# Two attention branches on one core: the second branch's third score pass as pairs of 64-row matmuls

## The chip, the cores and the metric

The kernel runs on one core of a Trainium2 chip. The metric is the device time of one execution in microseconds (us), the median of several runs. A core has a matrix engine (TensorE, PE in the profile), three engines for elementwise work (VectorE = DVE, ScalarE = ACT, GpSimd = POOL) and SyncE (SP), whose queue issues all of this kernel's copies (DMAs). Engines run side by side and wait for each other through semaphores. TensorE multiplies a stationary tile of up to 128 rows by 128 columns, put into its array by a weight load (PEld), with a moving tile of up to 512 columns, and adds the products in PSUM, in banks of 512 fp32 columns.

## What is computed

One encoder layer for 2048 prompt tokens and 512 sample tokens of width 1024. A wide input projection feeds two attention branches of eight heads each; both are gated, projected, merged and projected again (the tail). What the change touches is the second branch:

```python
qb = (rms_norm(bq, b_q_g) @ b_q_up).reshape(bsz, n, B_HEADS, B_NOPE + B_ROPE)
qb = concatenate([qb[..., :B_NOPE], apply_rope(qb[..., B_NOPE:], cos_b, sin_b)], axis=-1)
kv = (rms_norm(bkv, b_kv_g) @ b_kv_up).reshape(bsz, n, B_HEADS, B_NOPE + B_V)
kr = apply_rope(bkr.reshape(bsz, n, 1, B_ROPE), cos_b, sin_b)
kb = concatenate([kv[..., :B_NOPE], broadcast_to(kr, (bsz, n, B_HEADS, B_ROPE))], axis=-1)
vb = kv[..., B_NOPE:]
yb = block_attention(qb, kb, vb, (B_NOPE + B_ROPE) ** -0.5)
```

A key of this branch has 64 numbers of its own head and 32 (`kr`) shared by all heads. Each softmax is exact, with the row's maximum taken off.

## The kernel before, in words

Numbers are kept as pairs of a high part (rounded to the fp32r format; such a matmul has one record in the trace) and a low part (the rest), and a product is the sum of high x high, high x low and low x high.

**Stages.** `in_proj` (to about 1150 us) projects all tokens and stores q, k, v and gates. `attention` works through 80 jobs, `specs`: branch, head, chunk of 512 queries (four prompt chunks with 2048 keys, then one sample chunk with 512). `tail` does the rest. The first branch's jobs end at about 1944 us, the second's scores run from there to 2771.

**A job** is worked through in pairs of key tiles, 128 keys each: eight pairs for a prompt chunk, two for a sample chunk, so 272 pairs in each branch. For each pair `scores` (L969 to L989) takes a PSUM tile `st` of two banks (two such tiles exist), one bank for each key tile, and adds up 512 columns in each bank:

- first branch, two passes of 128 rows: `k1` x `qm`, `k2` x `qz`;
- second branch, three passes of 128 rows (L916): `k2` x `qm`, `k1` x `q1`, `k3` x `qz`.

In the third pass `k3` holds the high part of `kr` in rows 0 to 31, -1 in row 64 and zeros elsewhere; `qz` holds the low part of the query's rotary numbers in rows 0 to 31 and the query's maximum in row 64. So 33 of its 128 rows do work. ScalarE then takes the exponential twice (L983 rounded to `ph`, L984 in place), VectorE the difference `pl` (`lows`, L993), GpSimd adds up `ph` for the sums (L986). `values` (L996 to L1009), two steps later, multiplies `ph` and `pl` with the values `vt` (L1003, L1004), two matmuls for each key tile. `finish` copies the results out; VectorE's L1027 frees the bank for the next job's values.

**Maxima.** `max_stream` (L933 to L967) runs 12 to 13 steps ahead of the scores: for each step two matmuls `mp` (L947) and a reduction on VectorE (L950); at the end of a job a transpose (L959), and one step later `row` (L961) writes the maxima into row 64 of the job's `qz` by four small copies. That is some four steps ahead of the job's first scores.

**Order.** From L972 on, the order of every engine is written out by hand (`manual_schedule`). One step of the loop issues: the six (or four) score matmuls of a pair, one key tile (`values`), one step of the maxima, the second key tile, copies that are due, and `lows`. In a usual step of the second branch TensorE gets 6 + 2 + 4 = 12 matmuls. Copies go through SyncE's one queue in the order of issue; `later(n, f)` puts one off by n steps. `start_main` (L905) loads a job's `q1` and `qz` one or two jobs ahead, `load_k` (L801) the keys and values of a head five jobs ahead for the prompt. `k3` is loaded once for each of the two lengths (L826, L827), its memsets (L780, L781) run in the projection stage, and three `qz` are used in turn by both branches.

**Matmuls of fewer rows.** Two helpers in the projection stage, L264 and L464, multiply 4-row tiles with a 4x2 tile in plain fp32, each with two records in the trace; all other matmuls but one use all 128 rows. `sel[0]` x `acc` (L1008), at the end of each prompt job, is plain fp32 with 128 rows.

Of the kernel before, what the change touches and what calls it, by code (L numbers as in the profile page):

```python
# [10 lines left out]
F32R = mybir.dt.float32r  # L11
# [6 lines left out]
P = 128  # L18
# [14 lines left out]
def emit(tc, x_prompt, x_sample, c_prompt, c_sample, ada_w, ada_b, pre_g, post_g, w_in,  # L33
# [55 lines left out]
    with dram_cm as dram, const_cm as const:  # L89
# [27 lines left out]
        env = locals()  # L117
        h4 = in_proj(tc, nc, env)
        wt = attention(tc, nc, env, h4)
        tail(tc, nc, env, wt)  # L120

# [637 lines left out]
def attention(tc, nc, env, h4):  # L759
    e = NS(env)  # L760
    dma, nm, f32 = e.dma, e.nm, e.f32
    ha, fl, filler, cur, rest = h4
    kp = Pool(tc, "kp", "left")
# [12 lines left out]
        kv[0].append(kv_tiles(kp, NP_TOK, i))  # L776
    k3s = []
    for n in (NP_TOK, NS_TOK):
        k3 = kp.tile([P, n], F32R, name=f"k3{n}")
        nc.gpsimd.memset(f32(k3), 0.0)  # L780
        nc.gpsimd.memset(f32(k3[64:65, :]), -1.0)  # L781
        k3s.append(k3)
    qzs = []

# [16 lines left out]
    def load_k(br, kvh, smp, post):  # L801

        key = (br, kvh, smp)
        if key in kcur:
            return
        t0, n = (NP_TOK, NS_TOK) if smp else (0, NP_TOK)
        sl = slice(t0, t0 + n)
        k1, k2, vt = kv[smp][kcur["n"][smp] % len(kv[smp])]
        kcur["n"][smp] += 1
        rows = slice(64 * (kvh % 2), 64 * (kvh % 2) + 64)  # L810
        if br == 0:
            for s in range(2):
                post(k1[64 * s:64 * s + 64, :], e.ak_s[s][rows, sl])
            post(k2[0:64, :], e.ak_s[0][rows, sl])
            vsrc = e.va_s[sl, kvh, :]
        else:
            post(k2[0:64, :], e.bkn_s[0][kvh // 2, rows, sl])
            for s in range(2):
                post(k2[64 + 32 * s:96 + 32 * s, :], e.kr_s[s][:, sl])
            for s in range(2):  # L820
                post(k1[64 * (1 - s):64 * (1 - s) + 64, :], e.bkn_s[s][kvh // 2, rows, sl])
            vsrc = e.vb_s[sl, kvh, :]
        vsrc = vsrc.rearrange("(t p) d -> p t d", p=P)
        for t in range(0, n // P, 4):
            post(vt[:, t:t + 4, 0:P], vsrc[:, t:t + 4, :])
        if br == 1 and ("k3", smp) not in kcur:  # L826
            post(k3s[smp][0:32, :], e.kr_s[0][:, sl])  # L827
            kcur["k3", smp] = True
        kcur[key] = (k1, k2, vt)

# [6 lines left out]
    def q_src(br, h, c):  # L837
        sl = slice(c * CH, (c + 1) * CH)
        rows = slice(64 * (h % 2), 64 * (h % 2) + 64)
        return [s[h // 2, rows, sl] for s in (e.aq_s if br == 0 else e.bqn_s)], \  # L840
            [s[32 * h:32 * h + 32, sl] for s in e.bqr_s]

    def start(i, br, h, c):

        j = Job()
        j.br, j.h, j.c = br, h, c
        j.last = (br, h, c) == specs[-1]
        smp = int(c == 4)
        j.nk = (NS_TOK if smp else NP_TOK) // P
        j.direct = 0 if smp else j.nk // 2 - 1  # L850
        j.k1, j.k2, j.vt = kcur[(*kv_of(br, h), smp)]
        j.k3 = k3s[smp]
        qn, qr = q_src(br, h, c)
        j.qz = qzs[i % 3]
        j.qm = kp.tile([P, CH], F32R, tag="qm", name=nm("qm"), bufs=4)
        if br == 0:
            dma(f32(j.qm), qn[0].partition_broadcast(2))
            j.km = j.k1
            j.scale = SC_A
        else:  # L860
            dma(f32(j.qm[0:64, :]), qn[0])
            dma(f32(j.qm[64:128, :]), qr[0].partition_broadcast(2))
            j.km = j.k2
            j.scale = SC_B
        j.mx = kp.tile([P, 4, 2], F32, tag="mx", name=nm("mx"), bufs=3)
        return j
# [5 lines left out]
    def first():  # L872
        pieces = []
        load_k(0, 0, 0, lambda out, in_: pieces.append(lambda: post_now(out, in_)))

        def query():
            started[0] = start(0, 0, 0, 0)

        return pieces + [query]
# [5 lines left out]
    def mp_bank():  # L885
        return pp.tile([P, 2, CH], F32, tag="mp", name=nm("mp"), bufs=1)
# [18 lines left out]
    def start_main(i, br, h, c):  # L905

        qn, qr = q_src(br, h, c)
        qz = qzs[i % 3]
        if br == 0:
            dma(f32(qz[0:64, :]), qn[1])  # L910
            return lambda j, ks: ((j.k1[:, ks], j.qm), (j.k2[:, ks], qz))
        q1 = at.tile([P, CH], F32R, tag="q1", name=nm("q1"), bufs=3)
        for s in range(2):
            dma(f32(q1[64 * s:64 * s + 64, :]), qn[s])
        dma(f32(qz[0:32, :]), qr[1])
        return lambda j, ks: ((j.k2[:, ks], j.qm), (j.k1[:, ks], q1), (j.k3[:, ks], qz))  # L916

    jobs = []
    clock = [0]
# [2 lines left out]
    def later(steps, f):  # L922
        queue.append((clock[0] + steps, len(jobs), f))
        queue.sort(key=lambda q: q[0])
# [5 lines left out]
    def ahead(i):  # L930
        started[i] = start(i, *specs[i])

    def max_stream():  # L933

        for i, sp in enumerate(specs):
            j = started.pop(i, None) or start(i, *sp)
            jobs.append(j)
            long = j.nk > 4
            for n in range(pairs[i]):
                if n == 3 and i + 1 < len(specs):  # L940
                    ahead(i + 1)
                if n == 6 and i + 2 < len(specs) and pairs[i + 1] < 8:
                    ahead(i + 2)
                mp = mp_bank()
                for a in range(2):
                    qt, kc = (n // 2, 2 * (n % 2) + a) if long else (2 * n + a, 0)
                    nc.tensor.matmul(mp[:, a, :], lhsT=j.qm[:, qt * P:(qt + 1) * P],  # L947
                                     rhs=j.km[:, kc * CH:(kc + 1) * CH], start=True, stop=True)
                if long:
                    nc.vector.tensor_reduce(out=j.mx[:, n // 2, n % 2:n % 2 + 1], in_=mp.rearrange("p a k -> p (a k)"),  # L950
                                            axis=AX.X, op=ALU.max)
                else:
                    nc.vector.tensor_reduce(out=tops[i % 3][0][:, 2 * n:2 * n + 2], in_=mp, axis=AX.X, op=ALU.max)
                if n + 1 < pairs[i]:
                    yield True
            m, mt = tops[i % 3]
            if long:
                nc.vector.tensor_reduce(out=m[:, 0:4], in_=j.mx, axis=AX.X, op=ALU.max)
            nc.vector.transpose(out=mt, in_=m)  # L959

            def row(j=j, mt=mt):  # L961
                r = f32(j.qz[64:65, :]).rearrange("o (t b q) -> o t b q", b=4, q=32)
                for b in range(4):
                    dma(r[:, :, b, :], mt[32 * b:32 * b + 4, :])

            later(1, row)
            yield True  # L967

    def scores(j, n):  # L969

        if n == 0:
            if j.direct:  # L972
                j.acc = at.tile([P, 2, CH], F32, tag="acc", name=nm("acc"), bufs=2)
            j.hs, j.ls = [], []
        st = pp.tile([P, 2, CH], F32, tag="st", name=nm("st"), bufs=2)
        for a in range(2):
            kt = 2 * n + a
            ps = j.passes(j, slice(kt * P, (kt + 1) * P))
            for i, (k, q) in enumerate(ps):
                nc.tensor.matmul(st[:, a, :], lhsT=k, rhs=q, start=(i == 0), stop=(i == len(ps) - 1))  # L980
        h = at.tile([P, 2, CH], F32R, tag="ph", name=nm("ph"), bufs=6)
        j.hs.append(h)
        nc.scalar.activation(out=h, in_=st, func=AF.Exp, scale=j.scale)  # L983
        nc.scalar.activation(out=st, in_=st, func=AF.Exp, scale=j.scale)  # L984
        if 0 < n < j.direct:
            nc.gpsimd.tensor_tensor(out=j.acc, in0=f32(j.hs[0]) if n == 1 else j.acc, in1=f32(h), op=ALU.add)  # L986
            if n == j.direct - 1:
                nc.gpsimd.tensor_tensor(out=j.acc[:, 0, :], in0=j.acc[:, 0, :], in1=j.acc[:, 1, :], op=ALU.add)
        return st  # L989
# [55 lines left out]
    with contextlib.ExitStack() as order:  # L1045
# [12 lines left out]
        ha.close()  # L1058
        wt = Pool(tc, "wt", "right")
        passes = {0: start_main(0, *specs[0])}  # L1060
        order.close()
        order.enter_context(tc.manual_schedule(engines={eng.PE, eng.Activation, eng.DVE, eng.Pool, eng.SP}))
        ready, g = [], -1
        while g + 1 < len(steps) or ready:
            g += 1
            clock[0] = g
            st, rest = None, None
            if g < len(steps):
                i, n = steps[g]
# [25 lines left out]
                st = scores(jobs[i], n)  # L1095
                ready += [(g + BACK + (n == 0), jobs[i], 2 * n + a) for a in range(2)]
            now = sum(r[0] <= g for r in ready)
            for m in range(min(now, 3)):
                if m == 1:
                    advance(lead + g + 1)  # L1100
                _, j, kt = ready.pop(0)
# [226 lines left out]
```

## Time and profile before

| | |
|---|---|
| time, median of 3 runs | 3247.29 us (3246.39 to 3251.93) |
| the profiled execution's own time | 3247.96 us |
| its span, first to last instruction | 3246.2 us |
| second branch, first to last score matmul | 826.6 us |

How to read it: a page gives each engine's busy time and the span in 40 equal slices, a digit being the share in tenths (9: 90% or more; PEclk: TensorE's granted clock in tenths of full speed). The other views are taken from the same execution: stretches (after the columns named there come the share and the GB/s of the DMA engines), groups of equal instructions with their mean duration and the idle time ahead of them, waits by the one waited for, and the timeline (start, length, engine, line, operation, out<-in, stationary rows*columns, shape, count, and in brackets the idle time of that engine before it). "PE" is the matmul, "PEld" the weight load, "SPq" an issue by SyncE, "issue" idle time without a semaphore that explains it. A matmul's end is modelled, and matmuls overlap, so its length is longer than the distance to the next.

### The profile page before, as it was taken

What the parts mean: (1) busy time and instruction counts of PE and PEld (TensorE: products, weight loads), DVE (VectorE), ACT (ScalarE), POOL (GpSimd) and SP (SyncE); (2) the same over time, 40 slices, a digit from 0 to 9 for tenths busy, and PEclk for the clock granted to TensorE, in tenths of its full rate; (3) what the DMA queues carried; (4) which work ended last, traced back from release to release, by engine and by line L of the source; (5) the groups of instructions that cost most, each with busy time, mean ns of one, the idle gap of its engine ahead of it and who ended that gap; (6) DMA issues with size and microseconds to landing.
All of it is one profiled execution on the core that took longest, in us unless ns stands there. A gap on an engine that the chain in (4) does not pass through costs nothing. (4 is left out here: it accounts for less than half of the span.)

```text
span 3246.2 us, 41787 instructions
## 1 busy us (share of the span) xinstructions
PE 3150.9 (97%) x15214; PEld 2543.9 (78%) x15214; DVE 1970.9 (61%) x2521; ACT 1635.3 (50%) x2169; POOL 1727.2 (53%) x1044
## 2 busy tenths in 40 slices
PE   7999999999999999999999999999999999999999
PEld 6988889988889777666666677777776777789998
DVE  5742214422206128999999998888888887544343
ACT  5332224232323237777777876766666676421122
POOL 6422123421214237777777777666766667654443
PEclk9999999999999999999999999999999999999999
DMA  8445542355524751012111034432333222565552
GB/s 242 145 153 202 198 144 91 132 192 198 188 91 150 228 148 42 27 32 61 28 40 31 29 80 93 95 83 74 89 83 77 53 70 71 177 188 169 159 174 74
DMA packets 277521, 373.39 MB, mean 115 GB/s; under 512 B 30636, under 2 KB 184564, under 8 KB 274852
## 3 DMA queue, kind: packets, MB, share of 16 engines
q1 hardware_dynamic: 277316, 370.73, 38.3%
q8 instruction: 120, 1.97, 0.3%
q14 instruction: 85, 0.70, 0.1%
HBM read 251.52 MB, written 118.96 MB: 114 GB/s over the span
## 5 line engine op out<-in xcount | busy, mean ns | idle before, releaser
L986 POOL TENSOR_TENSOR acc<-acc,ph 128x1024 f32<-128x1024 f32 x320 | 768.9, 2403 | 89.0 <-ACT ph L983 76.3
L983 ACT ACTIVATE ph<-st 128x1024 fp32r<-128x1024 f32 x544 | 558.3, 1026 | 394.6 <-PE st L980 391.3
L950 DVE TENSOR_REDUCE mx<-mp 128x1 f32<-128x1024 f32 x512 | 625.8, 1222 | 200.5 <-PE mp L947 198.6
L993 DVE TENSOR_TENSOR pl<-st,ph 128x1024 fp32r<-128x1024 f32 x544 | 658.2, 1210 | 32.6 <-ACT st L984 32.6
L984 ACT ACTIVATE st<-st 128x1024 f32<-128x1024 f32 x544 | 555.3, 1021 | 0.0
L209 POOL TENSOR_TENSOR wl<-wraw,wh 128x1536 fp32r<-128x1536 f32 (+3 forms) x59 | 189.0, 3214 | 508.3 <-ACT wh L208 507.7
L980 PE MATMUL st<-qm,k 128*128 128x512 f32 x1024 | 434.6, 424 | 7.1 <-DVE pl L993 6.2
L1003 PE MATMUL pv<-ph,vt 128*128 128x512 f32 x1024 | 406.5, 397 | 29.9 <-DVE s L1027 29.9
L980 PE MATMUL st<-qz,k 128*128 128x512 f32 x1056 | 418.1, 396 | 0.0
L1004 PE MATMUL py<-pl,vt 128*66 128x512 f32 x1024 | 405.8, 396 | 0.0
L947 PE MATMUL mp<-k,qm 128*128 128x512 f32 x1024 | 323.9, 397 | 2.6 <-DVE mx L950 0.4
L604 PE MATMUL mm<-hh,wh 128*128 128x512 f32 x768 | 302.2, 394 | 0.0
L604 PE MATMUL mm<-hl,wh 128*128 128x512 f32 x768 | 301.8, 393 | 0.0
L604 PE MATMUL mm<-hh,wl 128*128 128x512 f32 x768 | 301.8, 393 | 0.0
L980 PEld LDWEIGHTS st<-qm,k 128*128 128x128 f32 x1024 | 194.0, 189 | 104.5 <-DVE pl L993 29.4
L1003 PEld LDWEIGHTS pv<-ph,vt 128*128 128x128 f32 x1024 | 193.5, 189 | 88.0 <-DVE s L1027 36.5
L947 PEld LDWEIGHTS mp<-k,qm 128*128 128x128 f32 x1024 | 190.0, 188 | 80.4 <-DVE mx L950 17.5
L986 POOL TENSOR_TENSOR acc<-ph,ph 128x1024 f32<-128x1024 f32 x64 | 152.9, 2389 | 183.3 <-ACT ph L983 172.3
L980 PEld LDWEIGHTS st<-qz,k 128*128 128x128 f32 x1056 | 200.0, 189 | 48.4 <-issue 7.4
L340 PE MATMUL mm<-wh,hh 128*128 128x384 f32 (+1 forms) x640 | 211.2, 330 | 5.7 <-DVE rp L80 3.9
L340 PE MATMUL mm<-wl,hh 128*128 128x384 f32 (+1 forms) x640 | 210.3, 329 | 0.0
L340 PE MATMUL mm<-wh,hl 128*128 128x384 f32 (+1 forms) x640 | 205.7, 330 | 0.0
(235 smaller groups left out, 5735.3 us busy)
## 6 DMA issues: line engine op xcount, KB each, us to landing
wraw<-in_w_in SPq DMA_DIRECT2D x46, 768.0 KB
x<-in_x_prompt SPq DMA_DIRECT2D x32, 512.0 KB
wada<-in_ada_w SPq DMA_DIRECT2D x24, 512.0 KB
raw<-in_w_in SPq DMA_DIRECT2D x48, 256.0 KB
vb<-uv SPq DMA_DIRECT2D x20, 512.0 KB
qm<-aqh SPq DMA_DIRECT2D x40, 256.0 KB
mt<-ma SPq DMA_DIRECT2D x40, 256.0 KB
mt<-mb SPq DMA_DIRECT2D x40, 256.0 KB
```

The lines of the kernel that those rows point to most:

```text
L209: eng.tensor_tensor(out=l[:, :, 0:n], in0=raw[:, :, 0:n], in1=f32(h[:, :, 0:n]), op=ALU.subtract)
L340: nc.tensor.matmul(ps[:, 0:n], lhsT=lt, rhs=rt, start=(i == 0), stop=(i == 23))
L604: nc.tensor.matmul(ps, lhsT=lt, rhs=rt[:, k, :], start=(i == 0), stop=(i == 23))
L947: nc.tensor.matmul(mp[:, a, :], lhsT=j.qm[:, qt * P:(qt + 1) * P], rhs=j.km[:, kc * CH:(kc + 1) * CH], start=True, stop=True)
L950: nc.vector.tensor_reduce(out=j.mx[:, n // 2, n % 2:n % 2 + 1], in_=mp.rearrange("p a k -> p (a k)"), axis=AX.X, op=ALU.max)
L980: nc.tensor.matmul(st[:, a, :], lhsT=k, rhs=q, start=(i == 0), stop=(i == len(ps) - 1))
L983: nc.scalar.activation(out=h, in_=st, func=AF.Exp, scale=j.scale)
L984: nc.scalar.activation(out=st, in_=st, func=AF.Exp, scale=j.scale)
L986: nc.gpsimd.tensor_tensor(out=j.acc, in0=f32(j.hs[0]) if n == 1 else j.acc, in1=f32(h), op=ALU.add)
L993: nc.vector.tensor_tensor(out=l, in0=st, in1=f32(j.hs[-1]), op=ALU.subtract)
L1003: nc.tensor.matmul(j.X, lhsT=j.vt[:, kt, 0:P], rhs=j.hs[n][:, a, :], start=st, stop=sp)
L1004: nc.tensor.matmul(y, lhsT=j.vt[:, kt, 64:VW], rhs=j.ls[n][:, a, :], start=st, stop=False)
```

## The change

The third pass is cut to 64 rows. `k3` is half as long: rows 0 to 63 hold the even key tiles and rows 64 to 127 the odd ones, each with `kr` in its first 32 rows and -1 in its 33rd. `qz` holds the same query data twice, in rows 0 to 32 and in rows 64 to 96, so there is one more copy of the rotary part and four more of the maxima for each job of the second branch. A pair's order of matmuls becomes: passes one and two of the first tile, passes one and two of the second, third pass of the first (rows 0 to 63), third pass of the second (rows 64 to 127). The first branch has two passes and keeps its order.

```diff
--- before.py
+++ after.py
@@ -776,9 +776,10 @@
         kv[0].append(kv_tiles(kp, NP_TOK, i))
     k3s = []
     for n in (NP_TOK, NS_TOK):
-        k3 = kp.tile([P, n], F32R, name=f"k3{n}")
+        k3 = kp.tile([P, n // 2], F32R, name=f"k3{n}")
         nc.gpsimd.memset(f32(k3), 0.0)
-        nc.gpsimd.memset(f32(k3[64:65, :]), -1.0)
+        for r in (32, 96):
+            nc.gpsimd.memset(f32(k3[r:r + 1, :]), -1.0)
         k3s.append(k3)
     qzs = []
 
@@ -824,7 +825,9 @@
         for t in range(0, n // P, 4):
             post(vt[:, t:t + 4, 0:P], vsrc[:, t:t + 4, :])
         if br == 1 and ("k3", smp) not in kcur:
-            post(k3s[smp][0:32, :], e.kr_s[0][:, sl])
+            tiles = e.kr_s[0][:, sl].rearrange("p (t two k) -> p t two k", two=2, k=P)
+            for a in range(2):
+                post(k3s[smp][64 * a:64 * a + 32, :].rearrange("p (t k) -> p t k", k=P), tiles[:, :, a, :])
             kcur["k3", smp] = True
         kcur[key] = (k1, k2, vt)
 
@@ -908,12 +911,19 @@
         qz = qzs[i % 3]
         if br == 0:
             dma(f32(qz[0:64, :]), qn[1])
-            return lambda j, ks: ((j.k1[:, ks], j.qm), (j.k2[:, ks], qz))
+            return lambda j, kt: [(j.k1[:, kt * P:(kt + 1) * P], j.qm), (j.k2[:, kt * P:(kt + 1) * P], qz)]
         q1 = at.tile([P, CH], F32R, tag="q1", name=nm("q1"), bufs=3)
         for s in range(2):
             dma(f32(q1[64 * s:64 * s + 64, :]), qn[s])
-        dma(f32(qz[0:32, :]), qr[1])
-        return lambda j, ks: ((j.k2[:, ks], j.qm), (j.k1[:, ks], q1), (j.k3[:, ks], qz))
+        for a in range(2):
+            dma(f32(qz[64 * a:64 * a + 32, :]), qr[1])
+
+        def passes(j, kt):
+            ks, half = slice(kt * P, (kt + 1) * P), slice(64 * (kt % 2), 64 * (kt % 2) + 64)
+            n = kt // 2
+            return [(j.k2[:, ks], j.qm), (j.k1[:, ks], q1), (j.k3[half, n * P:(n + 1) * P], qz[half, :])]
+
+        return passes
 
     jobs = []
     clock = [0]
@@ -959,9 +969,10 @@
             nc.vector.transpose(out=mt, in_=m)
 
             def row(j=j, mt=mt):
-                r = f32(j.qz[64:65, :]).rearrange("o (t b q) -> o t b q", b=4, q=32)
-                for b in range(4):
-                    dma(r[:, :, b, :], mt[32 * b:32 * b + 4, :])
+                for p in (64,) if j.br == 0 else (32, 96):
+                    r = f32(j.qz[p:p + 1, :]).rearrange("o (t b q) -> o t b q", b=4, q=32)
+                    for b in range(4):
+                        dma(r[:, :, b, :], mt[32 * b:32 * b + 4, :])
 
             later(1, row)
             yield True
@@ -973,11 +984,12 @@
                 j.acc = at.tile([P, 2, CH], F32, tag="acc", name=nm("acc"), bufs=2)
             j.hs, j.ls = [], []
         st = pp.tile([P, 2, CH], F32, tag="st", name=nm("st"), bufs=2)
-        for a in range(2):
-            kt = 2 * n + a
-            ps = j.passes(j, slice(kt * P, (kt + 1) * P))
-            for i, (k, q) in enumerate(ps):
-                nc.tensor.matmul(st[:, a, :], lhsT=k, rhs=q, start=(i == 0), stop=(i == len(ps) - 1))
+        ps = [j.passes(j, 2 * n + a) for a in range(2)]
+        last = len(ps[0]) - 1
+        order = [(a, i) for a in range(2) for i in range(2)] + [(a, i) for i in range(2, last + 1) for a in range(2)]
+        for a, i in order:
+            k, q = ps[a][i]
+            nc.tensor.matmul(st[:, a, :], lhsT=k, rhs=q, start=(i == 0), stop=(i == last))
         h = at.tile([P, 2, CH], F32R, tag="ph", name=nm("ph"), bufs=6)
         j.hs.append(h)
         nc.scalar.activation(out=h, in_=st, func=AF.Exp, scale=j.scale)
```

## Rows read from the trace of the kernel before

**Rows 1.** the page: TensorE's busy time and share; its granted clock in 40 slices.

```profile
...
PE 3150.9 (97%) x15214; PEld 2543.9 (78%) x15214; DVE 1970.9 (61%) x2521; ACT 1635.3 (50%) x2169; POOL 1727.2 (53%) x1044
...
PEclk9999999999999999999999999999999999999999
...
```

**Rows 2.** stretches, first, second branch: length, busy (count) PE PEld DVE ACT POOL, clock.

```profile
...
1308.00:1944.40 636.40, 618.10 (x2547) 442.76 (x2546) 596.32 (x583) 501.81 (x553) 485.92 (x233) 0.99 0.16 42
...
1944.40:2771.00 826.60, 806.73 (x3394) 603.29 (x3393) 672.58 (x652) 570.14 (x630) 571.51 (x272) 0.99 0.32 78
```

**Rows 3.** who TensorE's matmuls waited for, second branch: us, times, longest.

```profile
...
PE pv L1003 <- DVE s L1027: 14.2, 8, 1.8
PE st L980 <- DVE pl L993: 5.4, 2, 4.8
```

**Rows 4.** costliest groups, second branch: busy, mean ns, idle before, releaser.

```profile
...
L993 DVE TENSOR_TENSOR pl<-st,ph 128x1024 fp32r<-128x1024 f32 x272 | 329.1, 1210 | 25.3 <-ACT st L984 25.3
L950 DVE TENSOR_REDUCE mx<-mp 128x1 f32<-128x1024 f32 x245 | 299.6, 1223 | 116.7 <-PE mp L947 116.1
L983 ACT ACTIVATE ph<-st 128x1024 fp32r<-128x1024 f32 x271 | 278.1, 1026 | 249.6 <-PE st L980 248.2 <-POOL acc L986 0.8 <-POOL acc L988 0.5
...
```

**Rows 5.** timeline, one pair of the second branch: start, length, engine, line.

```profile
...
2203.02 0.39 PE L1003 MATMUL pv<-ph,vt 128*128 128x512 f32 x1
...
2204.41 0.40 PE L980 MATMUL st<-q,k 128*128 128x512 f32 x1
2204.41 0.19 PEld L980 LDWEIGHTS st<-qz,k 128*128 128x128 f32 x1
2204.64 0.39 PE L980 MATMUL st<-qz,k 128*128 128x512 f32 x1
...
2204.87 0.39 PE L1003 MATMUL pv<-ph,vt 128*128 128x512 f32 x1
...
```

**Rows 6.** timeline, gate projection: 512-column matmuls, 4-row ones, and back.

```profile
...
225.78 0.40 PE L604 MATMUL mm<-hl,wh 128*128 128x512 f32 x1
226.10 0.18 PEld L464 LDWEIGHTS tr<-comb,mrow 4*128 4x128 f32 x1 [0.37 <-issue]
226.11 0.27 PE L464 MATMUL tr<-comb,mrow 4*128 4x2 f32 x1
...
227.44 0.52 PEld L464 LDWEIGHTS tr<-comb,mrow 4*128 4x128 f32 x4
...
227.98 0.19 PEld L604 LDWEIGHTS mm<-hh,wl 128*128 128x128 f32 x1
227.98 0.50 PE L604 MATMUL mm<-hh,wl 128*128 128x512 f32 x1
...
228.32 0.40 PE L604 MATMUL mm<-hh,wh 128*128 128x512 f32 x1
...
```

**Rows 7.** timeline, weight loads: two other passages into 4-row matmuls.

```profile
...
31.49 0.52 PEld L264 LDWEIGHTS tr<-comb,row 4*128 4x128 f32 x4 [0.17 <-issue]
...
59.63 0.52 PEld L264 LDWEIGHTS tr<-comb,row 4*128 4x128 f32 x4 [0.17 <-issue]
...
```

**Rows 8.** timeline, end of a job: a 128-row matmul of the other format.

```profile
...
2206.50 0.39 PE L1006 MATMUL py<-ph,sel 128*66 128x512 f32 x1
2206.50 0.36 PEld L1008 LDWEIGHTS py<-acc,sel 128*66 128x66 f32 x2
...
```

**Rows 9.** row and query copies: durations of all; SyncE's timeline; first third pass.

```profile
...
L44 SPq DMA_DIRECT2D qz<-mt x320: 572/573/684, 1203.7 to 2743.8; - x160
...
2293.60 2.56 SPq L44 DMA_DIRECT2D qz<-mt  x4
...
2300.89 0.53 SPq L44 DMA_DIRECT2D qz<-bqrl  x1
...
2303.95 0.40 PE L980 MATMUL st<-qz,k 128*128 128x512 f32 x1
...
```

**Rows 10.** L780: duration in ns, min, median, max; first and last start.

```profile
...
L780 POOL MEMSET k<- x2: 523/1168/1812, 1050.5 to 1052.3; 128x2048 f32 x1, 128x512 f32 x1
...
```

## The prediction

> **What bounds the kernel now.** I read the page first: TensorE is marked busy for 97% of the span, no other engine for more than 61%, and the granted clock is at the top of its scale in every slice [rows 1]. A matmul's end is modelled, so that share alone proves little. Next I cut out the stretch the change touches, from the first score matmul of the second branch (1944.4) to the last (2771.0), and the pure part of the first branch for comparison [rows 2]. The second branch lasts 826.6 us for 8 x (4 x 8 + 2) = 272 pairs of key tiles, 3.04 us each. VectorE is busy 81% of it, ScalarE 69%, GpSimd 69%; in the first branch VectorE stood at 94%.
>
> The waits of TensorE settle it: in those 826.6 us it waited on another engine 10 times, 19.6 us in all [rows 3], while ScalarE waited 248 us for score matmuls and VectorE 116 us for the maxima's [rows 4]. So in the second branch TensorE's own stream sets the pace, and what is added to or taken from it reaches the end almost whole.
>
> The timeline gives the price of one matmul. From 2203.02 to 2204.87 there are eight steps of 512 columns in 1.85 us, 0.231 us each. The duration printed (0.39 to 0.40) is latency; the pitch is what counts. Each weight load starts when the matmul before it starts, and lies wholly beside it [rows 5].
>
> **What the change does to TensorE.** A pair has 12 matmuls of that pitch in its usual step: six scores, two maxima, four values. The change keeps the first two passes, moves both third passes to the end of the six and makes each a 64-row matmul, one on rows 0 to 63, one on rows 64 to 127. Count from the start of the last full score matmul to the start of the value matmul behind the scores.
>
> Before: three steps, 3 x 0.231 = 0.693 us.
>
> After, if the halves run side by side, one matmul of 0.231 goes. But the array passes from 128-row use to 64-row use and back in every pair. The second branch of the kernel before has no such passage, so I looked for matmuls of fewer rows. The nearest are in the input projection: 4-row matmuls straight behind 512-column ones [rows 6]. There the last full matmul starts at 225.78, and its successor would have started at 226.01. The 4-row weight load, which in the ordinary stream would have begun at 225.78, begins only at 226.10: 0.09 us after the columns have gone in, with no semaphore named ("issue"). It then lies bare: the way back shows what a bare load costs, since the full matmul printed at 227.98 is 0.50 long instead of 0.40 and its successor comes 0.34 later instead of 0.23, so 0.11 us. Way in: 0.09 + 0.11 = 0.20 us.
>
> On the way back the 4-row loads follow one another at 0.113 (four loads printed as 0.52 from 227.44, each 0.18 long, so the last begins at 227.78); the full load comes at 227.98, 0.20 behind it and thus 0.09 late, and again lies bare for 0.11. Way out: 0.20 us.
>
> Is it the number of rows, or the switch between the two fp32 formats? Two other passages into 4-row matmuls show the same idle load queue [rows 7], while a 128-row matmul of the other format, at the end of a job, has its load begin with the matmul before it, as usual [rows 8]. So it is the rows.
>
> The Trainium skill, TensorEngine Tiling (Array Packing), Key Properties, says that a change of tiling mode drains the engine. These rows show such a drain for 4 rows; that it also holds for halves of 64 rows no run here shows yet.
>
> Between the two halves there is a second load. On one and the same row block, loads with almost no matmul between them come 0.113 apart [rows 6]. The second half's load stands behind the first half's matmul in the queue, but goes to other rows. Bounds: 0 (it overlaps the first load) and 0.11 (it follows it, while the first half's matmul already runs). I take 0.11, since the only bare loads shown follow one another. The Trainium skill, TensorE: Matmul & The Clock Gate, Part 3, has packed tiles start some 4 ns apart; by that the lower bound would hold and the sum would be 3289.
>
> Sum after: 0.231 (the last full matmul) + 0.20 (in) + 0.11 (second load) + 0.231 (second half's columns) + 0.20 (out) = 0.972 us. Against 0.693 that is **+0.28 us a pair**, x 272 = +76 us; with the lower bound +0.17, or +46.
>
> A little is absorbed. Eight waits of 1.77 us behind the 2-pair jobs, 14.2 us in all [rows 3], are for VectorE; two slower pairs (0.56 us) come before each, so up to 8 x 0.56 = 4 us goes. Result: +72 us (bounds +42 and +72).
>
> **The rest of the edit.** Per second-branch job SyncE issues four more row copies and one more query copy: 4 x 0.573 + 0.53 = 2.8 us, x 40 = 113 us spread over 826. The rows of a job were issued from 2293.60, done at 2296.16, and the job's first third pass ran at 2303.95 [rows 9]. Finishing 2.3 us later leaves 5.5 us, and the third pass now comes later in its pair. Behind the rows stand loads of keys and queries for later jobs, which move by the same 2.8 us: several us to jobs ahead, so nothing. If that cover went, 40 jobs x up to 2.8 us = 113 us would show as TensorE waiting at a job's first pair. The key tile of the third pass is loaded in two copies instead of one, once for each of the two lengths, about 0.5 us of issue each, jobs ahead of its use. Its memset, 1.81 us for 2048 columns, becomes half as long, and the row of -1 becomes two of half the length; GpSimd runs them during the projection, at 1050 to 1055 [rows 10]: nothing either way. The first branch keeps its order, since it has two passes: nothing.
>
> The profiled execution took 3247.96 (span 3246.2 and 1.8 around it), 0.7 above the median of 3247.29. So 3247.3 + 72 = **3319 us**.
>
> **Rivals.**
> (a) The halves of 64 rows are entered and left without a drain: then a pair saves 0.231, 272 pairs save 63 us, and the time is 3185. For it: the load queue otherwise works ahead in every step [rows 5]; VectorE would rise to 672.6 / 764 = 88%, below the 94% it reached in the first branch [rows 2]. Against: rows 6 and 7. It decides as soon as in, out and second load together cost less than 0.231. The packing measurements in TensorE: Matmul & The Clock Gate of the Trainium skill would lead there; they time packs, and what rows 6 show is the passage between full and packed use. Chance 0.14.
> (b) Only the drain of 0.09 is paid each way and the loads are hidden: 0.231 + 0.09 + 0.231 + 0.09 = 0.642, that is -0.05 a pair, -14 us, 3233; with the second load bare +0.06, +16, 3263. Against: in rows 6 the load itself was late, not only the matmul. Chance 0.09, split over all three signs.
> (c) The halves do not overlap, so the change doesn't do what it says: 2 x 0.231 stay and 0.40 comes on top, +0.40 a pair, +109, less 4, 3352. Nothing in the trace excludes it. Chance 0.08.
> Forecast: chance 0.69.
>
> **How the numbers follow.** A measurement of this kernel tells 0.2%, or 6.5 us, from no change. Slower by more: the forecast, (c) and a part of (b), 0.79. Faster by more: (a) and a part of (b), 0.17. Within: 0.04. The forecast's own bounds are 3289 and 3319, with some 15 us either way for a drain of 64 rows that is shorter or longer than that of 4 rows (0.03 us at each of the two passages is 16 us). The range takes in (c) above and the slower part of (b) below: 3258 to 3356. It leaves out (a) and the faster part of (b).
>
> **What would show it.** In the profile after: (1) the weight load of the first 64-row matmul begins about 0.32 us after the start of the full matmul before it, not with it, and the load of the value matmul likewise after the second half; (2) the two halves' matmuls begin about 0.11 apart, with overlapping columns; (3) the stretch of the second branch is near 899 us instead of 826.6 with TensorE still the one that waits least; (4) the first branch and the tail are as before. Wrong would be: loads that begin with the matmul before them at both passages and a stretch near 764 (rival a); halves 0.23 apart or more (rival c); or third passes that wait for a row copy.

## The result and the profile after

| | before | after |
|---|---|---|
| time, median of 4 runs each | 3246.84 us (3244.35 to 3251.93) | 3292.23 us (3290.88 to 3294.07) |
| the profiled execution's own time | 3247.96 us | 3293.17 us |
| its span | 3246.2 us | 3291.3 us |
| second branch, first to last score matmul | 826.6 us | 871.3 us |

The changed kernel is slower: ratio 1.0138 [1.0121, 1.0156], 45.4 us by the medians. The stretch of the second branch alone grew by 871.3 - 826.6 = 44.7 us, so the whole difference is there: it begins at 1944.2 us after 1944.4, and what follows it takes 475.8 us (3291.3 - 2815.5) after 475.2. These are two lines of the page of the changed kernel, and that stretch (stretch; its length; busy us and count of PE, PEld, DVE, ACT, POOL; granted clock; DMA share; GB/s):

```profile
...
PE 3196.0 (97%) x15214; PEld 2472.9 (75%) x15214; DVE 1974.7 (60%) x2521; ACT 1637.3 (50%) x2169; POOL 1723.3 (52%) x1046
...
PEclk9999999999999999999999999999999999999999
...
```

```profile
...
1944.20:2815.50 871.30, 852.02 (x3394) 533.16 (x3392) 672.79 (x651) 572.66 (x630) 569.58 (x272) 0.99 0.31 77
...
```

TensorE has exactly as many matmuls as before (3394 in the stretch), 45 us more busy time, and 70 us less of weight loading on the record, while VectorE, ScalarE and GpSimd are busy for what they were [rows 2]. Its granted clock is at the top of its scale in every slice of the page. The groups of the stretch by form, weight loads first, then matmuls (busy us, mean ns of one | idle time of that engine ahead of them, and what ended it):

```profile
...
L1015 PEld LDWEIGHTS pv<-ph,vt 128*128 128x128 f32 x510 | 96.8, 190 | 86.5 <-issue 48.0 <-DVE s L1039 17.0 <-DVE mx L960 5.6
...
L992 PEld LDWEIGHTS st<-qz,k 64*128 64x128 f32 x544 | 50.7, 183 | 99.4 <-issue 96.5 <-DMA q<-bqnl 0.7 <-DMA qz<-mt 0.7
...
```

```profile
...
L992 PE MATMUL st<-qz,k 64*128 64x512 f32 x544 | 136.2, 496 | 0.0
...
```

The 544 loads of 64 rows take 183 ns each, yet keep the load queue busy for only 50.7 us and not for 544 x 0.183 = 99.6: all through the branch they run two at a time. Ahead of them the queue is idle for 99.4 us, 0.37 for each couple, 96.5 of it put down to "issue", which is time without a semaphore; ahead of the value matmuls' loads it is 86.5, where half of the group stands behind a couple, with 48.0 of it "issue". So on the way in it isn't another engine that is waited for, and on the way out for the larger part not either; the 17.0 us put down to VectorE's L1039 were 17.7 in the kernel before. The matmuls are 496 ns each on average, and 136.2 / 272 = 0.50 us is also what a couple takes, so the two begin and end together. The waits of TensorE's matmuls on other engines in the stretch agree (us, times, longest):

```profile
...
PE pv L1015 <- DVE s L1039: 14.5, 8, 1.8
PE st L992 <- DVE pl L1005: 4.8, 2, 4.5
```

That is as it was [rows 3]. The time went into TensorE's own stream, and the timeline of one pair shows where (start, length, engine, line, operation, out<-in, stationary rows*columns, shape, count, idle time of that engine before):

```profile
...
2202.07 0.40 PE L992 MATMUL st<-q,k 128*128 128x512 f32 x1
...
2202.39 0.19 PEld L992 LDWEIGHTS st<-qz,k 64*128 64x128 f32 x2 [0.36 <-issue]
2202.40 0.50 PE L992 MATMUL st<-qz,k 64*128 64x512 f32 x2
...
2202.83 0.19 PEld L1015 LDWEIGHTS pv<-ph,vt 128*128 128x128 f32 x1 [0.25 <-issue]
2202.83 0.50 PE L1015 MATMUL pv<-ph,vt 128*128 128x512 f32 x1
...
2203.17 0.39 PE L1016 MATMUL py<-pl,vt 128*66 128x512 f32 x1
...
```

The last full score matmul starts at 2202.07. In the kernel before, the next load began with it [rows 5]; here the load of the 64-row matmuls begins at 2202.39, 0.32 later. "x2" means that two loads share this row: both halves are loaded within 0.19 us, which is the length of a single load. The two matmuls share the next row. It is 0.50 long where one full matmul is 0.40, so the columns begin about 0.10 late, near 2202.50. The next load comes at 2202.83, 0.33 behind that, and is bare again: the value matmul's row is 0.50 long too, and its successor starts at 2203.17, which is 0.34 later and not 0.23.

From 2202.07 to the value matmul's effective start at 2202.94 (2203.17 less one pitch of 0.23) are 0.87 us. Before there were three steps in this place, 0.693. That is 0.18 a pair, x 272 = 48 us, against 44.7 measured. The pair shown is a little longer than most: over the trace's 272 pairs the median of the distance from the last full score matmul to the second value matmul is 1.091 us (1.10 in this pair), against 0.928 for the same four steps in the kernel before. That is 0.163 a pair, or 44 us. A lower clock in this profile, read in the last section, should add some 5 us to that, so a few us stay open.

### The profile page after: what moved, and what is told of

Same layout as the page of the kernel before. It is cut to its first block, busy times and chain, and to the rows that moved or that the text cites. A ratio compares the mean times of both kernels' runs of the same rounds, so it can differ in the third digit from the quotient of the medians.

```text
span 3291.3 us, 42164 instructions
## 1 busy us (share of the span) xinstructions
PE 3196.0 (97%) x15214; PEld 2472.9 (75%) x15214; DVE 1974.7 (60%) x2521; ACT 1637.3 (50%) x2169; POOL 1723.3 (52%) x1046
## 5 line engine op out<-in xcount | busy, mean ns | idle before, releaser
L960 DVE TENSOR_REDUCE mx<-mp 128x1 f32<-128x1024 f32 x512 | 625.9, 1222 | 240.9 <-PE mp L957 238.7
L1005 DVE TENSOR_TENSOR pl<-st,ph 128x1024 fp32r<-128x1024 f32 x544 | 658.1, 1210 | 26.7 <-ACT st L996 20.4
L1015 PE MATMUL pv<-ph,vt 128*128 128x512 f32 x1024 | 431.3, 421 | 30.2 <-DVE s L1039 30.2
L992 PE MATMUL st<-qz,k 64*128 64x512 f32 (+1 forms) x1056 | 339.2, 448 | 0.1
L992 PEld LDWEIGHTS st<-qz,k 64*128 64x128 f32 (+1 forms) x1056 | 147.7, 186 | 124.0 <-issue 104.4
```

Of the source, the lines that this page charges most:

```text
L1005: nc.vector.tensor_tensor(out=l, in0=st, in1=f32(j.hs[-1]), op=ALU.subtract)
L1015: nc.tensor.matmul(j.X, lhsT=j.vt[:, kt, 0:P], rhs=j.hs[n][:, a, :], start=st, stop=sp)
```

## The experiments

Each kernel is the changed one with the edit shown; the times are set against runs of the kernel before on the same chip, and the stretch against the 871.3 us of the changed kernel.

**All of the change but the 64-row matmuls.**

```diff
-        k3 = kp.tile([P, n // 2], F32R, name=f"k3{n}")
+        k3 = kp.tile([P, n], F32R, name=f"k3{n}")
-        for r in (32, 96):
+        for r in (32,):
-            tiles = e.kr_s[0][:, sl].rearrange("p (t two k) -> p t two k", two=2, k=P)
-            for a in range(2):
-                post(k3s[smp][64 * a:64 * a + 32, :].rearrange("p (t k) -> p t k", k=P), tiles[:, :, a, :])
+            post(k3s[smp][0:32, :], e.kr_s[0][:, sl])
-            return [(j.k2[:, ks], j.qm), (j.k1[:, ks], q1), (j.k3[half, n * P:(n + 1) * P], qz[half, :])]
+            return [(j.k2[:, ks], j.qm), (j.k1[:, ks], q1), (j.k3[:, ks], qz)]
```

> All of the change but the 64-row matmuls: the new order of the six score matmuls, the ten copies per job into qz and the smaller memsets are kept, the third passes are 128-row matmuls again (k3 at its old length, -1 in row 32, zeros in rows 33 to 127). Theory (the passage between 128-row and 64-row use is the whole cost): the time of the kernel before, 3247 us within 7. Rival (the added copies, or the order, make the pairs wait): near 3292 us.

Measured: 3249.99 us in 11 runs against 3248.6 in 15 of the kernel before, ratio 1.0004 [0.9995, 1.0013]. The stretch of this kernel:

```profile
...
1940.70:2770.60 829.90, 810.07 (x3394) 604.49 (x3393) 671.53 (x652) 570.01 (x630) 571.85 (x272) 0.99 0.33 81
...
```

It lasts 829.9 us and not 871.3. The new order of the passes and the doubled copies are all in here, so they cost nothing that can be measured: the medians differ by 1.4 us, within their interval, and the 3.3 us that this one profile's stretch has over the 826.6 of the kernel before fit the lower clock in it (3.5 us of full clock, last section). All of the loss belongs to the 64-row matmuls. Not in here are the halved memset of `k3` and its load in two copies; the second branch of the changed kernel begins 0.2 us earlier than before, so they delay nothing up to there. The copies were really made. This is the group of row copies in the profile of the changed kernel (durations in ns: least, median, most; first and last start):

```profile
...
L44 SPq DMA_DIRECT2D qz<-mt x480: 572/573/749, 1202.6 to 2790.9; - x160
...
```

There are 480 instead of 320, at the same 573 ns [rows 9]; the kernel of this experiment has 480 at 573 ns as well.

**Both halves on one row block.**

```diff
-            return [(j.k2[:, ks], j.qm), (j.k1[:, ks], q1), (j.k3[half, n * P:(n + 1) * P], qz[half, :])]
+            return [(j.k2[:, ks], j.qm), (j.k1[:, ks], q1), (j.k3[0:64, ks], qz[0:64, :])]
```

`k3` is of full length again, filled as in the kernel above.

> Both third passes of a pair on the same 64 rows (rows 0 to 63), copies as in the change. Theory (in the change the two halves stream side by side and only one matmul's columns count): the halves now follow each other, the second load hidden under the first half's columns, +0.23 us a pair on the change, x 272 = +63, 3355 us. Rival (the halves already follow one another in the change): 3292 us, no difference.

Measured: 3349.05 us, ratio 1.0308 [1.0292, 1.0324]. Its stretch, and its timeline of one pair:

```profile
...
1942.70:2872.40 929.70, 912.93 (x3394) 562.48 (x3392) 675.40 (x652) 573.15 (x630) 569.51 (x272) 0.99 0.29 72
...
```

```profile
...
2203.00 0.39 PE L990 MATMUL st<-q,k 128*128 128x512 f32 x1
...
2203.32 0.29 PEld L990 LDWEIGHTS st<-qz,k 64*128 64x128 f32 x2 [0.36 <-issue]
2203.32 0.73 PE L990 MATMUL st<-qz,k 64*128 64x512 f32 x2
...
2203.97 0.19 PEld L1013 LDWEIGHTS pv<-ph,vt 128*128 128x128 f32 x1 [0.36 <-issue]
2203.97 0.50 PE L1013 MATMUL pv<-ph,vt 128*128 128x512 f32 x1
...
```

The time is 6 us below the expected 3355, the stretch 58.4 us longer than in the changed kernel, 0.21 a pair. Now the two loads need 0.29 instead of 0.19, so the second comes 0.10 after the first. The two matmuls need 0.73 instead of 0.50, and the next load begins 0.65 after the first of the pair's two loads (2203.32 to 2203.97) instead of 0.44. On one block the matmuls follow each other; on two blocks they overlap. So the change does what it says, and rival (c) is out.

**Four passages instead of two in a pair.**

```diff
-        order = [(a, i) for a in range(2) for i in range(2)] + [(a, i) for i in range(2, last + 1) for a in range(2)]
+        order = [(a, i) for a in range(2) for i in range(last + 1)]
```

> The change with the old order of a pair: first tile's three passes, then the second tile's, so the array goes to 64 rows and back twice a pair, each time for one half. Theory (a visit costs 0.64 us, of which 0.23 are columns and 0.41 the two passages): +0.64 us a pair on the change, x 272 = +174, 3466 us. Rival (no passage cost, a 64-row matmul is itself slow, 0.32 us each): the same two matmuls, 3292 us.

Measured: 3450.5 us in one run. Its stretch, and its timeline:

```profile
...
1944.50:2974.70 1030.20, 1017.03 (x3394) 559.37 (x3392) 675.36 (x652) 573.48 (x630) 568.08 (x272) 0.99 0.27 65
...
```

```profile
...
2203.79 0.40 PE L992 MATMUL st<-q,k 128*128 128x512 f32 x1
2204.11 0.18 PEld L992 LDWEIGHTS st<-qz,k 64*128 64x128 f32 x1 [0.37 <-issue]
2204.12 0.49 PE L992 MATMUL st<-qz,k 64*128 64x512 f32 x1
...
2204.54 0.19 PEld L992 LDWEIGHTS st<-qm,k 128*128 128x128 f32 x1 [0.24 <-issue]
...
2204.88 0.40 PE L992 MATMUL st<-q,k 128*128 128x512 f32 x1
...
```

The stretch is 158.9 us longer than in the changed kernel, 0.58 a pair. A single half behind a full matmul shows the same signs as the couple: load 0.32 after the full matmul's start, matmul 0.49 long, next load 0.43 after its own. One visit from full rows to half rows and back costs this much whether one half goes or two: over the whole traces the median from the last full matmul to the second one behind the visit is 1.086 us with one half and 1.091 with two. The price sits in the passages and not in the matmuls. On the kernel before, this kernel adds 1030.2 - 826.6 = 203.6 us, 0.75 a pair, thus 0.37 for each of its two visits, each with the columns of one matmul as before. The time is 15 us below the expected 3466. Some 5 of them are shorter waits for VectorE (9.6 us in 8 instead of 14.5); another 5 would follow from a visit of 0.39 instead of the 0.41 expected (1.086 less three pitches of 0.231); the rest is open.

**Two couples in one visit.** A couple of 64-row matmuls whose stationary rows are zeros is put ahead of the third pass, so it adds nothing to the sum.

```diff
+    z3 = kp.tile([P, P], F32R, name="z3")
+    nc.gpsimd.memset(f32(z3), 0.0)
-            return [(j.k2[:, ks], j.qm), (j.k1[:, ks], q1), (j.k3[half, n * P:(n + 1) * P], qz[half, :])]
+            return [(j.k2[:, ks], j.qm), (j.k1[:, ks], q1), (z3[half, :], qz[half, :]),
+                    (j.k3[half, n * P:(n + 1) * P], qz[half, :])]
```

> The change with one more couple of 64-row matmuls a pair (stationary zeros, same moving tile), right ahead of the third passes, so two couples in one visit to 64-row use. Theory (cost per visit, not per 64-row matmul; within a visit a couple costs one matmul of 0.23): +63 us on the change, 3355 us. Rival (a couple costs 0.64 whenever it comes): +174, 3466 us. If the loads of a couple are bare inside a visit too: +0.11 more a pair, 3385 us.

Measured: 3348.5 us, ratio 1.0309 [1.0295, 1.0323]. Its stretch, and its timeline:

```profile
...
1942.00:2870.10 928.10, 911.38 (x3938) 561.62 (x3936) 675.21 (x652) 573.19 (x630) 569.87 (x272) 0.99 0.30 72
...
```

```profile
...
2204.32 0.40 PE L995 MATMUL st<-q,k 128*128 128x512 f32 x1
...
2204.65 0.19 PEld L995 LDWEIGHTS st<-qz,z 64*128 64x128 f32 x2 [0.37 <-issue]
2204.65 0.50 PE L995 MATMUL st<-qz,z 64*128 64x512 f32 x2
...
2204.76 0.19 PEld L995 LDWEIGHTS st<-qz,k 64*128 64x128 f32 x2
2204.98 0.40 PE L995 MATMUL st<-qz,k 64*128 64x512 f32 x2
2205.31 0.19 PEld L1018 LDWEIGHTS pv<-ph,vt 128*128 128x128 f32 x1 [0.37 <-issue]
...
2205.66 0.39 PE L1019 MATMUL py<-pl,vt 128*66 128x512 f32 x1
...
```

The time is 6 us below the expected 3355, the stretch 56.8 us longer than in the changed kernel, 0.21 a pair: the second couple costs no more than one full matmul does, and has no second visit to pay. Its loads begin at 2204.76, beside the first couple's matmuls, and its matmuls print 0.40 from 2204.98, the ordinary length. Within a visit the load queue works ahead as in the full stream.

**Two couples that replace four full matmuls.** If the price is one of visits, a visit pays from its second couple on. Here the second pass runs as halves too, with 64 of its 128 rows.

```diff
-            return [(j.k2[:, ks], j.qm), (j.k1[:, ks], q1), (j.k3[half, n * P:(n + 1) * P], qz[half, :])]
+            return [(j.k2[:, ks], j.qm), (j.k1[half, ks], q1[half, :]), (j.k3[half, n * P:(n + 1) * P], qz[half, :])]
-        order = [(a, i) for a in range(2) for i in range(2)] + [(a, i) for i in range(2, last + 1) for a in range(2)]
+        full = 2 if j.br == 0 else 1
+        order = [(a, i) for a in range(2) for i in range(full)] + [(a, i) for i in range(full, last + 1) for a in range(2)]
```

> The change with the second pass cut to 64 rows as well (rows 0 to 63 for the first tile, 64 to 127 for the second; half of that pass's sum is left out of the scores), in the same visit: four full score matmuls fewer than the kernel before, two couples in one visit. Theory (a visit costs 0.41 us whatever is in it, a couple in it 0.21 to 0.23): against the change two matmuls of 0.231 go and one couple comes, -0.23 to -0.25 us a pair, x 272 = -63 to -69, 3223 to 3229 us, below the kernel before: a visit pays from the second couple on. Rival (the cost lies in the couple, 0.64 each): +0.18 a pair, 3341 us. Rival (VectorE or a wait becomes the bound once TensorE gains): no lower than the kernel before, 3247 us.

Measured: 3236.83 us against 3248.75 of the kernel before, ratio 0.9964 [0.995, 0.9978]. Its stretch, its timeline, and TensorE's longest wait:

```profile
...
1939.60:2758.30 818.70, 796.83 (x3394) 464.10 (x3392) 671.88 (x652) 570.12 (x630) 568.51 (x272) 0.98 0.33 82
...
```

```profile
...
2202.32 0.63 PE L993 MATMUL st<-qm,k 128*128 128x512 f32 x2
...
2202.88 0.19 PEld L993 LDWEIGHTS st<-q,k 64*128 64x128 f32 x2 [0.37 <-issue]
2202.88 0.50 PE L993 MATMUL st<-q,k 64*128 64x512 f32 x2
...
2203.21 0.39 PE L993 MATMUL st<-qz,k 64*128 64x512 f32 x2
...
2203.54 0.19 PEld L1016 LDWEIGHTS pv<-ph,vt 128*128 128x128 f32 x1 [0.36 <-issue]
...
2203.88 0.39 PE L1017 MATMUL py<-pl,vt 128*66 128x512 f32 x1
...
```

```profile
...
PE pv L1016 <- DVE s L1040: 16.4, 8, 2.1
...
```

The sign turned: this kernel is faster than the one before, by 0.4%, so both rivals (3341, and no lower than 3247) are out. It is still 8 us above the expected 3223 to 3229. It leaves work out, so it is no version to use; it shows where the balance lies. The first row holds two full matmuls, 0.63 long, so the last one starts at 2202.55 (0.23 after 2202.32). From there to the value matmul's effective start (2203.88 - 0.23 = 2203.65) are 1.10 us, against 0.87 with one couple: the second couple costs 0.23 and saves two full matmuls, 0.46. By that the stretch should be 0.23 x 272 = 63 us shorter than the changed kernel's; it is 52.6 shorter. Some 2 of the missing 10 us are the longer waits (16.4 instead of 14.5), and about 5 are a lower clock, which the last section reads; the rest stays open.

No version that computes everything and beats the kernel before came out of this. The second pass needs all its 128 rows, so there is only one couple a pair. Two pairs in one visit would save 4 x 0.231 and cost 2 x 0.23 + 0.40, an estimated 0.03 us a pair, and would hold both tiles `st` at once. Cutting all full matmuls of the branch into halves, with no passage left, was not tried either: both row blocks would have to add into one bank of PSUM in turn.

## Why the prediction came out as it did

**The bound: right.** TensorE's own stream sets the pace of the second branch, and what was added to it reached the end: +44.7 us in the stretch, +45.4 in the medians.

**The drain and the bare load: right, both ways.** Taken from the 4-row passage [rows 6], they were 0.09 + 0.11 each way. With 64 rows the load begins 0.32 after the full matmul's start, just as there, so 0.09 after its columns have gone in. On the way out the couple's columns run from about 2202.50 to 2202.73, and the load comes at 2202.83, 0.10 later, and is bare for 0.11. By the median of all pairs the two ways come to 1.091 - 3 x 0.231 = 0.40 us, as the sum had it. The price came from 4-row matmuls in the other fp32 format; here the 64-row matmuls and their neighbours are all fp32r, so the rows bring the passage and not the format. The drain that the Trainium skill, TensorEngine Tiling (Array Packing), Key Properties, states for a change of tiling mode is now shown for 64 rows as well. Rivals (a) and (b) are out with this: (a) has no idle load queue, and in (b) the loads would be hidden, while the value matmul prints 0.50 and its successor comes 0.34 later.

**The second load: the term that was wrong.** I took 0.11 us for it, because the only bare loads shown follow one another; the bounds were 0 and 0.11. It is as good as 0: both loads share one row of 0.19, and in the trace's nanoseconds the two loads, and the two matmuls, begin 3 to 4 ns apart in each of the 272 couples. That alone is 0.11 x 272 = 30 us and makes +46 of the +76. The rows I took the price from were loads on one and the same row block, and the experiment on one block shows that there the second does come 0.10 later. The price was right for its case, which is not this case. The Trainium skill, TensorE: Matmul & The Clock Gate, Part 3, whose packed tiles start some 4 ns apart, had the better value, and its sum of 3289 is 3 us from the 3292 measured (3293 without the 4 us taken off wrongly, see below); the trace agrees, with its 3 to 4 ns. So sign (2), halves 0.11 apart, was wrong too; sign (1) held, and in (3) the stretch was 871 and not 899.

**The 4 us absorbed: wrong.** I let the slower pairs eat into VectorE's waits behind the 2-pair jobs. They are 14.5 us in 8 waits, after 14.2 [rows 3]. The trace shows why. The end of a 2-pair job in the kernel before, then in the changed one:

```profile
...
2159.85 0.63 PE L947 MATMUL mp<-k,qm 128*128 128x512 f32 x2
...
2163.65 0.51 PE L1003 MATMUL pv<-ph,vt 128*128 128x512 f32 x1 [1.79 <-DVE s L1027]
...
```

```profile
...
2169.24 0.62 PE L957 MATMUL mp<-k,qm 128*128 128x512 f32 x2
...
2169.90 1.23 DVE L960 TENSOR_REDUCE mx<-mp 128x1 f32<-128x1024 f32 x1 [1.72 <-PE mp L957]
...
2173.03 0.50 PE L1015 MATMUL pv<-ph,vt 128*128 128x512 f32 x1 [1.83 <-DVE s L1039]
...
```

In the changed kernel VectorE had itself waited 1.72 us for TensorE's maxima matmuls. Then come its L960, L1005 and L1039, and TensorE goes on 3.79 us after the first of the two maxima matmuls; in the kernel before that was 3.80 (2159.85 to 2163.65), and in all five experiments it is 3.79 to 3.81. So what came earlier moves VectorE along. The wait gives way only to what TensorE does after those maxima, and that is the scores of one pair, not of two. Up to the wait these hold the way in and one pitch less, +0.20 - 0.231, so the wait grew by 0.03 (1.79 to 1.83); the way out falls inside it. The other kernels agree: with two halves in turn or two couples in that place the waits are 1.6 us each, with two visits 1.2, and in the last experiment, which has one pitch less there than the changed kernel, 2.05. By this the eight waits hide some 8 x 0.163 = 1.3 us and not 4.

**What was costed at nothing: right.** Order and doubled copies together moved the time by a ratio of 1.0004, and the start of the second branch shows no cost of the other memsets and loads of `k3`. Sign (4) held by the same numbers: the first branch ends as before, and the tail takes 475.8 us after 475.2.

The forecast of 3319 was thus 27 us high: 30 for the load, less 4 for the waits, and 1 in the rest.

## What to carry to other kernels

Packing two half-height matmuls into the array saves one matmul a couple, but each visit from full rows to half rows and back has its own price; here that was a drain of 0.1 us and a bare load of 0.11 us on the way in and again on the way out, 0.40 us together over all pairs, against 0.23 saved for a couple. So count the couples in one visit before you cut rows: one couple lost 0.16 us a pair, two would win a little, and scattering the halves over more visits made it worse. And when a price is taken from far rows, ask what those rows share with the case and what not: here the passage carried over from 4 rows to 64, the distance of loads on one row block did not carry over to two. And a wait doesn't take up a slowdown that comes before the event on which the awaited engine itself waits.

## What was not expected of the hardware

**Loads on two row blocks cost one.** Two 64-row loads took 0.19 us together on two blocks, beginning 3 to 4 ns apart, and 0.29 on one.

**The granted clock fell after short waits, more often in some executions.** In the changed kernel TensorE waited 1.83 us for VectorE, from 2171.20 to 2173.03. Stretches of 2 us of that kernel (columns as above, clock third from the end):

```profile
...
2170.00:2172.00 2.00, 1.20 (x6) 0.49 (x4) 2.00 (x2) 2.00 (x4) 2.00 (x1) 1.00 0.00 0
2172.00:2174.00 2.00, 0.97 (x4) 0.79 (x5) 0.94 (x2) 1.35 (x2) 1.05 (x2) 1.00 0.00 1
2174.00:2176.00 2.00, 2.00 (x6) 1.36 (x6) 1.49 (x3) 0.00 (x0) 2.00 (x2) 0.53 0.22 47
2176.00:2178.00 2.00, 2.00 (x7) 0.91 (x6) 1.21 (x2) 0.00 (x0) 0.72 (x1) 0.61 0.09 19
2178.00:2180.00 2.00, 2.00 (x11) 1.49 (x10) 0.81 (x1) 1.92 (x2) 0.76 (x1) 1.00 0.01 1
...
```

TensorE works for 0.97 us in the window in which the wait ends. In the next two the granted clock is 0.53 and 0.61, so it stands at the lower level (1.2 GHz, half of 2.4) for most of both, and the engine is busy throughout with 6 and 7 matmuls. Then the clock is back at 1.00, with 11 matmuls in the window. The kernel before had a wait of 1.79 us at 2163.65 as well, but no dip behind it. Two 50-us windows of the kernel before, the second one with a dip:

```profile
...
2150.00:2200.00 50.00, 48.21 (x206) 35.95 (x205) 40.44 (x39) 33.89 (x39) 33.52 (x16) 1.00 0.52 120
...
2350.00:2400.00 50.00, 48.23 (x198) 35.83 (x197) 39.26 (x40) 33.53 (x38) 28.97 (x16) 0.97 0.44 95
...
```

And two of the last experiment:

```profile
...
2150.00:2200.00 50.00, 47.95 (x204) 28.40 (x203) 39.54 (x39) 33.86 (x38) 34.38 (x17) 0.97 0.53 124
...
2450.00:2500.00 50.00, 42.98 (x169) 24.90 (x168) 39.38 (x38) 30.19 (x37) 28.06 (x14) 0.90 0.41 89
...
```

Of the 16 such windows from 1950 to 2750, three are below 1.00 in the kernel before (all 0.97), four in the first experiment, five in the changed kernel (four 0.97, one 0.93) and eight in the last experiment (six 0.97, one 0.90, one 0.99). Summed, that is 0.09, 0.16, 0.19 and 0.29 of 50 us in the kernel before, the first experiment, the changed kernel and the last experiment, or 4.5, 8, 9.5 and 14.5 us of full clock. So about 5 us of what the last experiment missed are there. The number of 64-row matmuls doesn't explain it: the second, third and fourth experiments, which have as many or more, show four, two and three such windows. What does differ in the last experiment is the length of the eight waits, 2.05 us instead of 1.8 (16.4 in sum). The clock fell within 1.5 us of the end of seven of them, of four of eight in the changed kernel and of two of eight in the kernel before, where they are 0.03 us shorter than in the changed one. Whether the longer waits are the cause, or whether executions differ by this much anyway, these single profiles can't tell.
